# The low parts of the weights in a two-block network: from two engines to VectorE alone

## The chip, the core and the metric

The kernel runs on 1 core of one Trainium2 chip, in one launch. The metric is the device time of one execution in microseconds, as the median of repeated runs. The engines are named as in the profile: PE is TensorE (PEld its weight loads), DVE is VectorE, ACT is ScalarE, POOL is GpSimd, and SP is SyncE, which issues the loads.

## What is computed

Two networks of two layers each, on 256 tokens of width 1024 in float32. The first block's layer has one large input projection and three mixers whose outputs are gated and summed; the second block's layer has two feed-forward parts around a convolution mixer (layer 0) or a latent attention (layer 1), each with an attention over a memory of 256 tokens.

```python
def first_block(x, ...):
    for l in range(DEPTH):
        h = rmsnorm(x, norm_g[l])
        proj = h @ w_in[l]
        (a_q, a_ff, a_fb, a_i, a_g, b_q, b_k, b_v, b_g, c_s, c_g, merge) = jnp.split(proj, IN_OFFSETS, axis=-1)
        y_a = hgrn2_mixer(a_q, a_ff, a_fb, a_i, lbs[l], hgrn_norm_g[l]) * jax.nn.silu(a_g)
        y_b = retention_mixer(b_q, b_k, b_v, ret_norm_g[l], ret_norm_b[l]) * jax.nn.silu(b_g)
        y_c = rwkv7_mixer(c_s, ...) * jax.nn.silu(c_g)
        gates = jax.nn.sigmoid(merge.reshape(b, t, 3, D_MODEL))
        mixed = (gates[:, :, 0] * (y_a @ w_branch_a[l]) + gates[:, :, 1] * (y_b @ w_branch_b[l])
                 + gates[:, :, 2] * (y_c @ w_branch_c[l]))
        x = x + mixed @ w_out[l]
    return rmsnorm(x, final_norm_g)

def second_block(x, mem, ...):
    for layer in range(DEPTH):
        x = x + 0.5 * swiglu(rms_norm(x, norm_g[layer, 0]), ffn_w13[layer, 0], ffn_w2[layer, 0])
        h = rms_norm(x, norm_g[layer, 1])
        # layer 0: short_conv_mixer(h), layer 1: causal_mla_attention; both with memory_attention
        x = x + jnp.concatenate([y_mix, y_mem], axis=-1) @ w_out[layer]
        x = x + 0.5 * swiglu(rms_norm(x, norm_g[layer, 2]), ffn_w13[layer, 1], ffn_w2[layer, 1])
    return x
```

## The kernel before

**Layout.** Activations lie feature by feature: eight blocks of 128 features, 256 tokens each. Every projection runs over the weights in pieces of 128 x 256 features times a token width of 256.

**Three matmuls for one.** A float32 operand is split into a high part (rounded to the format `F32R`) and a low part (what the rounding left), and `mm3` (lines 343 to 347) adds up low x high, high x low and high x high, each a 128x128 by 128x256 matmul. The activations are split once and used by all weights. The weights are split as they arrive.

**The stream of weights.** `wload` (lines 327 to 341) is a generator that `fm` and `tm` (lines 349 and 364) draw on. It loads one chunk of 512 KB from HBM through the SP queue into a tile `raw` (three buffers), and treats it in pieces of 128x512: ScalarE casts the piece to its high part `whi` (line 386), and one of two engines subtracts that from the piece, which gives the low part `wlo` (line 387). A running number `nw` counts the pieces; each third piece is subtracted on GpSimd, the other two on VectorE. The high and low parts have four buffers each in a pool `whi`; in the first block a second pool `whx` of three buffers takes three pieces of each seven. One piece feeds twelve matmuls. Lines 386 and 387 stand in the helper `split`, which also splits activations, always on VectorE.

**What sets the order.** Each engine works through its own list of instructions in order. The kernel records its instructions as generators woven together by `weave` (line 39): in a layer of the first block, projections fill TensorE between the steps of four chains (the operands, the recurrences and the outputs of the third mixer, and the heads of the other two). The framework's scheduler then sets each engine's list when the program is built, by priority and by its own estimate of when an operand is ready; the lists are fixed when the kernel runs. The casts and subtractions of the weights are recorded 80 places ahead (`high_priority(80)`), the recurrences' element-wise steps 50 places ahead (`Ahead`, line 69).

**The chains that the text names.** `hgrn_head` (line 1200) makes the decay products of one head: exponentials on ScalarE, products on VectorE (`Z`, lines 1249 and 1250; `E`, lines 1242 and 1247) and small matmuls (`ppt`, line 1271); GpSimd adds the diagonal blocks into `P` (line 1280), and the matmul `hpo` (line 1181) uses it. `rwkv_states` (line 934) inverts triangular blocks by a chain of small matmuls (`pw`, `px`, lines 1018 and 1026) with VectorE between them (`W`, `XY`), and steps the state (`ch`, lines 1065, 1072 and 1081, with `UV` from VectorE). `bkP` (line 929) and `Pc` (lines 910, 911) are made on GpSimd. `rps` (line 1335) takes the rotated queries and keys `qk` from VectorE. `columns` (line 392) turns sums of squares into reciprocal roots by ten short dependent instructions on VectorE (`rs`, lines 411 to 425, the last on line 430 into `ycol`); `stat` (line 1470) runs it where the second block goes from one part to the next, and TensorE spreads the result (`psn`, line 445). `ffn` (line 1490) holds most of the second block's matmuls; its product `g` on line 1503 reads PSUM.

**Helpers.** Line 80 is the call within `Ahead`, so that many instructions of the recurrences carry this line.

Of the kernel before, what the change touches and what calls it, by code (L numbers as in the profile page):

```python
# [281 lines left out]
class Core:  # L282
# [44 lines left out]
    def wload(s, src, kt, n):  # L327

        nc = s.nc
        raw = s.raw.tile([128, 1024], F32, tag="raw", name="raw")  # L330
        nc.sync.dma_start(out=raw[:, :kt * n], in_=src)
        step = 512 // n
        for j in range(0, kt, step):
            c = min(step, kt - j)
            part = raw[:, j * n:(j + c) * n]
            s.nw += 1
            pool = s.whx if s.whx is not None and s.nw % 7 < 3 else s.whi
            hi, lo = (pool.tile([128, 512], F32R, tag=t, name=t)[:, :c * n] for t in ("whi", "wlo"))
            with s.tc.high_priority(80):
                s.split(hi, lo, part, s.nc.gpsimd if s.nw % 3 == 0 else None)  # L340
            yield j, c, hi.rearrange("p (k n) -> p k n", k=c), lo.rearrange("p (k n) -> p k n", k=c)

    def mm3(s, out, ah, al, bh, bl, start, stop):
# [1490 lines left out]
```

## Time and profile before

| | |
|---|---|
| median of 3 runs | 2808.9 us (2807.02 to 2813.55) |
| the profiled execution | 2819.39 us |
| its span, first to last instruction | 2817.6 us |
| TensorE, matmuls | 2662.0 us, 94% |
| VectorE | 1946.3 us, 69% |
| ScalarE | 1488.4 us, 53% |
| GpSimd | 917.1 us, 33% |
| mean granted clock of TensorE | 0.977 of full speed |
| moved by DMA | 385.41 MB, 137 GB/s |

A busy time is the sum over an engine's instructions, with what runs on top of each other counted once. The first block takes about the first 1770 us (its first layer 0 to 890, its second up to 1770), the second block the rest.

### The profile page before, as it was taken

Reading aid. Unit: us, or ns where it says so; the run is one execution under the profiler, and the core shown is the slowest. Engines: PE = TensorE matmul, PEld = TensorE weight load, DVE = VectorE, ACT = ScalarE, POOL = GpSimd, SP = SyncE. Lnnn points to the kernel's source line nnn. Section 1 sums busy time; section 2 is a strip of 40 time slices with the busy share of each in tenths; the row PEclk is TensorE's granted clock in tenths of the full one; section 3 lists DMA queues with packets and bytes.
Section 4 is the critical chain, followed back from the end, with each engine's and each line's share of the span. In section 5 each row is a group of like instructions: output and inputs, shape, how many; then the busy total and the mean of one; then the engine's idle time right before and its main releaser. Section 6 shows DMA issues by size and latency. Waiting matters only on the chain.

```text
span 2817.6 us, 76691 instructions
## 1 busy us (share of the span) xinstructions
PE 2662.0 (94%) x32003; PEld 2508.6 (89%) x32003; DVE 1946.3 (69%) x4045; ACT 1488.4 (53%) x2964; POOL 917.1 (33%) x868
## 2 busy tenths in 40 slices
PE   7898999999998899899999999999999999999999
PEld 7788888989998788788888999999899999997999
DVE  7878778776666977789776666755665665665654
ACT  6555555544455655555444445645455555545554
POOL 4333333322344433334233235222222322221222
PEclk9999999999999999999999999999999999998999
DMA  5333332333455333332333345555445554542555
GB/s 175 116 104 102 106 99 84 108 118 110 139 168 176 110 121 106 99 103 80 109 124 112 113 145 183 187 172 184 146 165 183 182 177 165 165 147 67 172 182 163
DMA packets 111804, 385.41 MB, mean 137 GB/s; under 512 B 12384, under 2 KB 16992, under 8 KB 111200
## 3 DMA queue, kind: packets, MB, share of 16 engines
q1 hardware_dynamic: 111024, 379.86, 41.7%
q8 instruction: 251, 4.11, 0.6%
q14 instruction: 97, 0.79, 0.1%
q10 hardware_dynamic: 432, 0.64, 0.1%
HBM read 378.36 MB, written 2.10 MB: 135 GB/s over the span
## 4 chain that ended last, share of the span: by engine, by line
PE 64%; DVE 11%; ACT 4%; issue 4%; POOL 3%; DMA 2%; ACTq 0%; POOLq 0%; DVEq 0%
PE pj L345 5%; PE pj L347 4%; PE pj L346 4%; PE pg L345 3%; PE pg L347 3%; PE pg L346 3%; PE pw L345 3%; PE pw L347 3%; PE pw L346 3%; PE pu L345 3%; PE pu L347 3%; PE pu L346 3%; DVE wlo L387 2%; PE pb L345 2%; PE pb L346 2%
## 5 line engine op out<-in xcount | busy, mean ns | idle before, releaser
L386 ACT CAST whi<-raw 128x512 fp32r<-128x512 f32 (+1 forms) x1407 | 858.4, 617 | 819.9 <-PE pj L347 230.7
L387 POOL TENSOR_TENSOR wlo<-raw,whi 128x512 fp32r<-128x512 f32 (+1 forms) x469 | 632.0, 1348 | 1534.2 <-ACT whi L386 1308.4
L387 DVE TENSOR_TENSOR wlo<-raw,whi 128x512 fp32r<-128x512 f32 x938 | 710.2, 762 | 441.1 <-ACT whi L386 436.2
L345 PE MATMUL pj<-hb,wlo 128*128 128x256 f32 x1408 | 431.5, 307 | 3.9 <-DVE wlo L387 1.6
L346 PE MATMUL pj<-hb,whi 128*128 128x256 f32 x1408 | 406.9, 289 | 0.7 <-DVE hb L387 0.7
L347 PE MATMUL pj<-hb,whi 128*128 128x256 f32 x1408 | 405.3, 288 | 0.6 <-issue 0.6
L345 PEld LDWEIGHTS pj<-hb,wlo 128*128 128x128 f32 x1408 | 273.4, 194 | 17.0 <-DVE wlo L387 1.9
L346 PEld LDWEIGHTS pj<-hb,whi 128*128 128x128 f32 x1408 | 274.2, 195 | 3.1 <-DVE hb L387 1.5
L347 PEld LDWEIGHTS pj<-hb,whi 128*128 128x128 f32 x1408 | 273.8, 195 | 2.0 <-issue 0.8
L345 PE MATMUL pg<-hs,wlo 128*128 128x256 f32 x704 | 200.2, 284 | 1.4 <-DVE x L493 1.1
L345 PE MATMUL pu<-hs,wlo 128*128 128x256 f32 x704 | 201.1, 286 | 0.3 <-POOL wlo L387 0.2
L347 PE MATMUL pu<-hs,whi 128*128 128x256 f32 x704 | 200.6, 285 | 0.0
L346 PE MATMUL pu<-hs,whi 128*128 128x256 f32 x704 | 200.4, 285 | 0.0
L345 PE MATMUL pw<-g,wlo 128*128 128x256 f32 x704 | 199.5, 283 | 0.0
L346 PE MATMUL pg<-hs,whi 128*128 128x256 f32 x704 | 199.5, 283 | 0.0
L347 PE MATMUL pg<-hs,whi 128*128 128x256 f32 x704 | 199.4, 283 | 0.0
L346 PE MATMUL pw<-g,whi 128*128 128x256 f32 x704 | 199.2, 283 | 0.0
L347 PE MATMUL pw<-g,whi 128*128 128x256 f32 x704 | 199.2, 283 | 0.0
L345 PE MATMUL pb<-hs,wlo 128*128 128x256 f32 x512 | 150.3, 293 | 1.6 <-DVE gb L847 1.6
L347 PE MATMUL pb<-hs,whi 128*128 128x256 f32 x512 | 145.0, 283 | 0.0
L346 PE MATMUL pb<-hs,whi 128*128 128x256 f32 x512 | 145.0, 283 | 0.0
L345 PEld LDWEIGHTS pu<-hs,wlo 128*128 128x128 f32 x704 | 136.2, 193 | 1.1 <-POOL wlo L387 0.7
(524 smaller groups left out, 7099.7 us busy)
## 6 DMA issues: line engine op xcount, KB each, us to landing
raw<-in_win SPq DMA_DIRECT2D x292, 512.0 KB, 3.6
raw<-in_w SPq DMA_DIRECT2D x256, 512.0 KB, 3.8
raw<-in_wbb SPq DMA_DIRECT2D x32, 512.0 KB, 3.5
raw<-in_wo SPq DMA_DIRECT2D x32, 512.0 KB, 3.6
raw<-in_wconv SPq DMA_DIRECT2D x20, 512.0 KB, 3.5
raw<-in_wba SPq DMA_DIRECT2D x16, 512.0 KB, 3.5
raw<-in_wbc SPq DMA_DIRECT2D x16, 512.0 KB, 3.7
raw<-in_lora SPq DMA_DIRECT2D x16, 256.0 KB, 2.8
```

What stands on the lines that cost most here:

```text
L345: mm(out=out, lhsT=al, rhs=bh, start=start, stop=False)
L346: mm(out=out, lhsT=ah, rhs=bl, start=False, stop=False)
L347: mm(out=out, lhsT=ah, rhs=bh, start=False, stop=stop)
L386: s.nc.scalar.copy(dh, src)
L387: (eng or s.nc.vector).tensor_tensor(dl, src, dh.bitcast(F32), ALU.subtract)
```

## The change

In `wload`, the choice of the engine is dropped: all 1407 subtractions go to VectorE, which `split` uses where no engine is named. The counter `nw` stays, since it also chooses the pool.

```diff
--- before.py
+++ after.py
@@ -337,7 +337,7 @@
             pool = s.whx if s.whx is not None and s.nw % 7 < 3 else s.whi
             hi, lo = (pool.tile([128, 512], F32R, tag=t, name=t)[:, :c * n] for t in ("whi", "wlo"))
             with s.tc.high_priority(80):
-                s.split(hi, lo, part, s.nc.gpsimd if s.nw % 3 == 0 else None)
+                s.split(hi, lo, part)
             yield j, c, hi.rearrange("p (k n) -> p k n", k=c), lo.rearrange("p (k n) -> p k n", k=c)
```

The scheduler sets VectorE's and GpSimd's lists anew. TensorE's list stays as it was, but for shifts by a few matmuls.

VectorE, first layer, at the first head (`Z` and `E` are the head's, `W`, `XY` and `bk` the third mixer's, `g` a gate). Before:

```order
L926 TENSOR_TENSOR bk<-bk,enL 128x8x64
L1247 TENSOR_TENSOR E<-S_991 128x2x4x32
L80 TENSOR_TENSOR W<-pw,c_127 128x256
L387 TENSOR_TENSOR wlo<-raw,whi 128x512
L1249 TENSOR_TENSOR Z<-kf,E 128x2x4x32
L1250 TENSOR_TENSOR Z<-q,E 128x256
L820 SCALAR_TENSOR_TENSOR g<-g,pj 128x512
L80 TENSOR_TENSOR XY<-XY,px 128x256
L1242 TENSOR_TENSOR E<-S_991 128x2x2x64
```

And now:

```order
L926 TENSOR_TENSOR bk<-bk,enL 128x8x64
L1247 TENSOR_TENSOR E<-S_991 128x2x4x32
L80 TENSOR_TENSOR W<-pw,c_127 128x256
L387 TENSOR_TENSOR wlo<-raw,whi 128x512
L1249 TENSOR_TENSOR Z<-kf,E 128x2x4x32
L1250 TENSOR_TENSOR Z<-q,E 128x256
L820 SCALAR_TENSOR_TENSOR g<-g,pj 128x512
L80 TENSOR_TENSOR XY<-XY,px 128x256
L387 TENSOR_TENSOR wlo<-raw,whi 128x512
L80 STREAM_TRANSPOSE XY<-XY 128x256
L1242 TENSOR_TENSOR E<-S_991 128x2x2x64
```

Up to line 1250 the list is the same; the further subtraction stands behind `XY`.

VectorE, second block, the statistics chain before the second feed-forward part of layer 0. Before:

```order
L418 TENSOR_SCALAR rs<-rs 128x2
L387 TENSOR_TENSOR wlo<-raw,whi 128x512
L419 TENSOR_TENSOR rs<-rs 128x2
L420 TENSOR_TENSOR rs<-rs 128x2
L421 SCALAR_TENSOR_TENSOR rs<-rs 128x2
L422 TENSOR_TENSOR rs<-rs 128x2
L423 TENSOR_TENSOR rs<-rs 128x2
L424 TENSOR_SCALAR rs<-rs 128x2
L425 TENSOR_TENSOR rs<-rs 128x2
L430 SCALAR_TENSOR_TENSOR ycol<-rs 128x2
```

And now:

```order
L387 TENSOR_TENSOR wlo<-raw,whi 128x512
L418 TENSOR_SCALAR rs<-rs 128x2
L419 TENSOR_TENSOR rs<-rs 128x2
L420 TENSOR_TENSOR rs<-rs 128x2
L421 SCALAR_TENSOR_TENSOR rs<-rs 128x2
L422 TENSOR_TENSOR rs<-rs 128x2
L387 TENSOR_TENSOR wlo<-raw,whi 128x512
L423 TENSOR_TENSOR rs<-rs 128x2
L424 TENSOR_SCALAR rs<-rs 128x2
L425 TENSOR_TENSOR rs<-rs 128x2
L430 SCALAR_TENSOR_TENSOR ycol<-rs 128x2
```

The chain now holds a second subtraction, between lines 422 and 423; the first moved ahead of line 418.

GpSimd, first layer, from the first `bkP` on. Before:

```order
L929 TENSOR_TENSOR bkP<-bk,Pc 128x512 x2
L387 TENSOR_TENSOR wlo<-raw,whi 128x512
L1171 TENSOR_SCALAR kf<-lf 128x2x256
L387 TENSOR_TENSOR wlo<-raw,whi 128x512 x2
L1221 TENSOR_TENSOR EK<-kf,EK 128x512
L387 TENSOR_TENSOR wlo<-raw,whi 128x512 x2
L1259 TENSOR_TENSOR cm<-cm 128x2x32
L1260 TENSOR_TENSOR cm<-cm 128x2x32
```

And now:

```order
L1171 TENSOR_SCALAR kf<-lf 128x2x256
L929 TENSOR_TENSOR bkP<-bk,Pc 128x512 x2
L1221 TENSOR_TENSOR EK<-kf,EK 128x512
L1259 TENSOR_TENSOR cm<-cm 128x2x32
L1260 TENSOR_TENSOR cm<-cm 128x2x32
```

Five subtractions stood between these instructions; none is left, and `kf` has moved ahead of `bkP`.

## Rows read from the trace of the kernel before

**Rows 1.** The page, busy time of each engine

```profile
PE 2662.0 (94%) x32003; PEld 2508.6 (89%) x32003; DVE 1946.3 (69%) x4045; ACT 1488.4 (53%) x2964; POOL 917.1 (33%) x868
```

**Rows 2.** Stages: length, busy us (instructions) by engine, PEclk, DMA share, GB/s

```profile
0.00:550.00 550.00, 494.30 (x8001) 449.78 (x8002) 442.51 (x1001) 310.40 (x647) 191.47 (x229) 0.96 0.34 111
900.00:1420.00 520.00, 479.52 (x7907) 435.67 (x7906) 429.02 (x946) 302.37 (x630) 188.11 (x209) 0.97 0.33 104
1770.00:2818.00 1048.00, 1015.63 (x8138) 987.98 (x8137) 614.13 (x1214) 546.84 (x1012) 281.15 (x215) 0.98 0.51 164
```

**Rows 3.** What ended waits of PE: us in total, times, longest us

```profile
PE hpo L1181 <- POOL P L1280: 12.5, 7, 3.2
PE pj L345 <- DVE wlo L387: 12.5, 2, 10.9
PE ch L1081 <- DVE UV L80: 8.7, 8, 2.2
PE pw L1018 <- DVE XY L80: 8.1, 9, 2.8
PE psn L445 <- DVE ycol L430: 7.7, 6, 2.9
PE ppt L1271 <- DVE Z L1250: 5.0, 2, 2.5
PE rps L1335 <- DVE qk L1292: 4.9, 3, 2.1
```

**Rows 4.** The page, costliest groups: count, busy us, mean ns, idle before, releaser

```profile
L387 POOL TENSOR_TENSOR wlo<-raw,whi 128x512 fp32r<-128x512 f32 (+1 forms) x469 | 632.0, 1348 | 1534.2 <-ACT whi L386 1308.4
L387 DVE TENSOR_TENSOR wlo<-raw,whi 128x512 fp32r<-128x512 f32 x938 | 710.2, 762 | 441.1 <-ACT whi L386 436.2
```

**Rows 5.** The subtractions: duration in ns min/median/max, first and last start

```profile
L387 POOL TENSOR_TENSOR wlo<-raw,whi x469: 995/1295/4017, 12.0 to 2808.0; 128x512 fp32r<-128x512 f32 x156, 128x384 fp32r<-128x384 f32 x1
L387 DVE TENSOR_TENSOR wlo<-raw,whi x938: 546/692/1807, 10.2 to 2806.5; 128x512 fp32r<-128x512 f32 x187, 128x384 fp32r<-128x384 f32 x1
```

**Rows 6.** Timeline of DVE near the start: start us, us, instruction and count

```profile
26.02 1.89 DVE L387 TENSOR_TENSOR wlo<-raw,whi 128x512 fp32r<-128x512 f32 x3
```

**Rows 7.** Rows 2's first stage, only instructions that read or write wlo

```profile
0.00:550.00 550.00, 256.60 (x833) 163.68 (x833) 110.36 (x141) 100.72 (x70) 0.96 0.34 111
```

**Rows 8.** Lines 1250 and 1503: the group as in rows 4, then as in rows 5

```profile
L1250 DVE TENSOR_TENSOR Z<-q,E 128x256 f32<-128x256 f32 x80 | 41.2, 515 | 1.5 <-ACT E L1245 0.9 <-ACT E L1244 0.5
L1250 DVE TENSOR_TENSOR Z<-q,E x80: 375/417/1490, 90.9 to 1351.6; 128x256 f32<-128x256 f32 x80
L1503 DVE TENSOR_TENSOR g<-si,pu x44: 673/687/690, 1791.2 to 2749.7; 128x512 f32<-128x512 f32 x44
```

**Rows 9.** Timeline of DVE and POOL at three places, as in rows 6

```profile
105.00 1.48 DVE L1250 TENSOR_TENSOR Z<-q,E 128x256 f32<-128x256 f32 x1
104.75 1.44 POOL L387 TENSOR_TENSOR wlo<-raw,whi 128x512 fp32r<-128x512 f32 x1
...
1099.86 3.42 DVE L387 TENSOR_TENSOR wlo<-raw,whi 128x512 fp32r<-128x512 f32 x2
1099.62 3.12 POOL L387 TENSOR_TENSOR wlo<-raw,whi 128x512 fp32r<-128x512 f32 x2
...
2086.41 0.69 DVE L387 TENSOR_TENSOR wlo<-raw,whi 128x512 fp32r<-128x512 f32 x1 [0.84 <-ACT whi L386]
2087.01 0.15 DVE L419 TENSOR_TENSOR rs<-rs 128x2 f32<-128x2 f32 x1
2087.99 1.24 DVE L424 TENSOR_SCALAR rs<-rs 128x2 f32<-128x2 f32 x1
2087.93 1.27 POOL L387 TENSOR_TENSOR wlo<-raw,whi 128x512 fp32r<-128x512 f32 x1 [4.65 <-ACT whi L386]
```

**Rows 10.** What ended waits before the subtractions, as in rows 3

```profile
DVE wlo L387 <- ACT whi L386: 436.2, 363, 4.4
POOL wlo L387 <- ACT whi L386: 1308.4, 351, 25.2
```

## The prediction

> **What bounds the kernel now.** I read four things in this order: the busy times, the stages, the instructions that the change touches, and the waits of TensorE. TensorE is busy for 2662.0 us of a span of 2817.6 us [rows 1], so 155.6 us is all that any edit off TensorE can win, unless it also brings back the granted clock. The windows [rows 2] show where that lies. In the two stretches in which the recurrences of the first block run beside the projections, TensorE is idle for 55.7 us of 550 and 40.5 us of 520, its granted clock is 0.96 and 0.97, and VectorE is busy for 442.5 us (80%) and 429.0 us (83%). In the second block (the last 1048 us) TensorE is idle for only 32.4 us. What to see: TensorE is the bound, and what it loses it loses where VectorE is fullest.
>
> The low parts of the weights are not what TensorE waits for: on them it waited twice, 10.9 of 12.5 us at the start [rows 3]. Its other long waits end on instructions of the recurrences, the attention heads and the statistics: five groups that VectorE releases hold 34.4 us in 28 waits (8.7 + 8.1 + 7.7 + 5.0 + 4.9 us), 1.23 us each, and one that GpSimd's additions to P release holds 12.5 us in 7. So the question is not when a low part is ready, but what its subtraction does to the two in-order queues that feed those waits.
>
> **The change, part by part.** GpSimd loses 469 subtractions of 1348 ns mean, 632.0 us of its 917.1 us; VectorE, which has 938 of them at 762 ns mean, makes 1407 [rows 1, 4].
>
> *What VectorE pays.* One subtraction lasts 692 ns at the median [rows 5], but they overlap at their ends: three in a row took 1.89 us [rows 6], so each further one costs (1.89 - 0.69) / 2 = 0.60 us. 469 x 0.60 = 281 us. Of the 469, 70 fall into the first dense stretch [rows 7].
>
> *What VectorE gets back.* The two engines hold each other up. VectorE's subtractions have a median of 692 ns and a mean of 762, with a longest of 1807 [rows 4, 5]; 938 x 0.070 = 66 us is excess. The product for the heads (line 1250, two operands in SBUF) has a median of 417 and a mean of 515 ns, which gives 80 x 0.098 = 8 us, while the product of line 1503, one operand of which lies in PSUM, never exceeds 690 ns [rows 8]. So the excess is there where both operands are in SBUF. Low end: these two groups alone, 74 us. High end: all of VectorE's 1946.3 us at their rate: 74 us on 938 x 0.692 + 80 x 0.417 = 682 us is 11%, which makes 1946.3 x 0.11 / 1.11 = 193 us. The subtractions are 632.0 of GpSimd's 917.1 us, 69%, so 51 to 133 us goes with them. I take the high end, because short instructions of serial chains are hit by as much as long ones: line 424 took 1.24 us where its neighbour on line 419 took 0.15 [rows 9].
>
> Net, VectorE gains 281 - 133 = 148 us of work and stands at 2094 us, 74% of the span; in the first dense stretch it goes from 442.5 to 442.5 + 70 x (0.60 - 0.28) = 465 us, 84%, the 0.28 being 133 / 469.
>
> The Trainium skill, page "SBUF — State Buffer", section "Who interferes with whom", gives a stricter rule: a VectorE instruction with two SBUF inputs and a GpSimd instruction that reads SBUF exclude each other, and the later one is blocked until the first has finished. By that rule every one of the 469 would cost VectorE half of its 1.295 us median, 0.65 us, if an instruction were always there to be blocked, 304 us in all, and the net would be a gain of 23 us instead of 148 us more work; rows 9 agree with the full block (1.24 us under a GpSimd subtraction of 1.27 us), the means agree with far fewer meetings.
>
> *What of it lies on the path.* Work on VectorE that no TensorE wait follows is hidden by 2662 us of matmuls. What counts is the few microseconds of VectorE's queue ahead of a wait. I read three such places. Ahead of a head's matmuls in the first layer, line 1250 took 1.48 us instead of its 0.417, and GpSimd's subtraction of 1.44 us ran beside it: 1.06 us. Ahead of a step of the recurrence in the second layer, two subtractions took 3.42 us where two at the 0.60 pitch take 1.29: 2.13 us, beside two of GpSimd's in 3.12 us. In a statistics chain of the second block, line 424 lost 1.24 - 0.15 = 1.09 us [rows 9]. So a hit costs 1.06 to 2.13 us there, against 0.60 for a subtraction that joins the queue, and the new order does not put one in everywhere: at the first place none more stands ahead of line 1250, in the statistics chain there is one more. GpSimd's seven waits of 12.5 us carry no such hit that I can name; they stay.
>
> I take it that half of the 28 shown waits carry a hit, of 1.23 us at most (the mean wait, since a wait can't give more than its length): 14 x 1.23 = 17 us. They pay half a subtraction each (one more at one of two places): 28 x 0.5 x 0.60 = 8 us. Net 9 us. The five groups are 34.4 of the 155.6 us of idle time; with the start and GpSimd's 12.5 us set aside, I count another third of that sum as alike, and come to 12 us. Both halves are choices. Low end of the cost: every hit goes and nothing is paid, and the rest of the dense stretches follows, 35 us won. High end: nothing is won at the waits, and the 8 us, scaled alike to 11, are paid.
>
> *Other edits, at nothing.* ScalarE makes the same 1407 high parts. The SP queue issues the same loads, and a raw buffer comes free at the end of a 0.69 us subtraction instead of a 1.3 us one. TensorE's order stays but for shifts of a few matmuls. Low parts are covered now, but for the start, by the weights that TensorE still has ahead of it [rows 3]; if that cover went, each late one would cost up to the 0.60 us.
>
> **The sum.** 2819.4 us for the profiled execution less 12 is 2807. That execution is 0.4% above the median of the runs shown, 2808.9; I set the same 12 us against the median: **2797 us**, 0.4% faster.
>
> **Rivals.**
>
> *Nothing that can be told (0.24).* Where a hit goes, the next instruction that the same matmul needs ends last: a table load or an exponential on ScalarE, or GpSimd's remaining 285 us, which hold VectorE as before. For it: the chains pass through all three engines, and seven waits end on GpSimd already [rows 3]. Against: the waits are short, 1.23 us, and a hit of 1.06 is most of one. Time: 2809. (About 0.2%, 6 us, is what a measurement of this kernel can tell from no change.)
>
> *Slower: VectorE's queue stands (0.22).* A subtraction can't start before ScalarE's cast, which waits for TensorE to release a buffer. VectorE stood before its subtractions for 436.2 us in 363 waits, 1.20 us each, at 39% of the 938; GpSimd stood there 1308.4 us at no cost [rows 10]. With 469 more, 39% of them make 181 further waits, 218 us, and whatever stands behind in VectorE's queue stands too. The place: the statistics chain, where VectorE already waited 0.84 us before a subtraction in the middle of ten dependent instructions [rows 9], and the new order sets one more into that chain. Against: both queues are ordered so that mostly nothing that is ready stands behind. At 80 to 84% of the dense stretches VectorE also has time left to stand in. Price: if one in eight of the 181 is ahead of a TensorE wait, 27 us, less the 12: 2824. It decides from 12 / 218, one in 18.
>
> The Trainium skill, page "Perfetto Trace Analysis", section "Optimizing Scalar/DVE Operations", speaks for this side: handing work to GpSimd can make sense if VectorE is saturated, though the shared port may spoil it. By that rule the change would cost the 27 us if VectorE counted as saturated; at 80 to 84% of the dense stretches the trace does not bear that out.
>
> *A larger gain (0.16).* GpSimd's queue, rid of subtractions that waited 1308.4 us in it, starts its additions, products and gate sums at once; the 12.5 us of waits on P go, as do the hits, and with shorter gaps the granted clock, 0.96 to 0.97 in the dense stretches, rises by a hundredth there (1% of 1070 us, 11 us). 12 + 12.5 + 11 = 35 us: 2774. Against: at those waits GpSimd's own instructions are what runs.
>
> *The change doesn't do what it says* can be left out: no line 387 is left in GpSimd's order.
>
> **How the numbers follow.** Forecast 0.38, larger gain 0.16, nothing 0.24, slower 0.22. Faster by over 0.2% is 0.38 + 0.16 = 0.54, same 0.24, slower 0.22. For the range I leave out some 0.08 of the larger gain below 2772 and some 0.1 of the slower case above 2826: 2772 to 2826. The forecast's own range is 2786 to 2803.
>
> **What would show it.** Right: VectorE's subtractions number 1407 with a mean below 715 ns; its busy time is 2060 to 2130 us; GpSimd's about 285; TensorE's busy time stays at 2662 within 10 us, and its idle time in the dense stretches falls below the 96 us of now; line 424 in the statistics chain is back under 0.2 us. Wrong on the price: VectorE's time before its subtractions goes well beyond 436 us and the waits of TensorE on the statistics and the recurrences grow. Wrong on the cause: the hits go and TensorE's idle time stays at 155 us. A time above 2826 or under 2772 would mean a mechanism that I have not seen.

## The result, and the profile after

The change makes the kernel faster: 2745.3 us (2738.64 to 2755.29) against 2814.1 us (2807.02 to 2818.74), a ratio of 0.9756 with a 95% interval of 0.9738 to 0.9774. That is 69 us, where 12 were forecast, and it lies below the range. The profiled execution took 2752.12 us, with a span of 2750.3.

The page's busy times of the changed kernel and its group of the subtractions, which answer to [rows 1, 4]:

```profile
PE 2649.6 (96%) x32003; PEld 2502.5 (91%) x32003; DVE 2070.4 (75%) x4514; ACT 1489.5 (54%) x2964; POOL 299.1 (11%) x399
...
L387 DVE TENSOR_TENSOR wlo<-raw,whi 128x512 fp32r<-128x512 f32 (+1 forms) x1407 | 983.2, 707 | 419.9 <-ACT whi L386 410.3
```

VectorE makes 1407 low parts and is busy for 124.1 us more; GpSimd is busy for 618 us less. Of the 67.3 us by which the span is shorter, TensorE's busy time gives 12.4 and its idle time 54.9 (155.6 to 100.7).

The stages, cut where TensorE has done the same matmuls, to within one, as in [rows 2] (columns as there):

```profile
0.00:526.70 526.70, 487.57 (x8001) 445.10 (x8002) 449.87 (x1071) 308.84 (x648) 95.94 (x159) 0.97 0.36 115
867.20:1379.50 512.30, 483.33 (x7908) 439.77 (x7908) 428.94 (x1020) 301.67 (x630) 101.86 (x142) 0.96 0.33 107
1721.50:2750.30 1028.80, 1009.56 (x8137) 984.91 (x8136) 696.91 (x1429) 549.55 (x1012) 0.00 (x0) 0.99 0.53 166
```

In the first stage VectorE carries 70 instructions more and is busy for 7.4 us longer; the second has 74 more in the same time. The stages take 23.3, 7.7 and 19.2 us less, and TensorE's idle time in them falls from 55.7 to 39.1, 40.5 to 29.0 and 32.4 to 19.2 us.

What ended waits of TensorE, the lines that answer to [rows 3], and the largest of the others:

```profile
PE hpo L1181 <- POOL P L1280: 13.6, 6, 3.6
PE pj L345 <- DVE wlo L387: 13.4, 4, 10.9
PE pw L1018 <- DVE XY L80: 7.6, 8, 3.2
PE px L1026 <- DVE W L80: 4.7, 5, 1.8
PE pn L453 <- DVE SC L80: 4.3, 4, 2.2
...
PE rps L1335 <- DVE qk L1292: 2.6, 4, 0.8
...
PE ppt L1271 <- DVE Z L1250: 1.8, 2, 1.4
...
PE ch L1081 <- DVE UV L80: 0.8, 1, 0.8
...
PE psn L445 <- DVE ycol L430: 0.3, 2, 0.2
```

`UV`, `ycol`, `Z` and `qk` gave back much of what they held, but `XY` and `P` hardly anything. These rows are only a part of it, and [rows 3] is a choice from its view: four groups that VectorE releases stand in the same view, as long as those chosen.

```profile
PE psn L405 <- DVE acc L468: 8.1, 6, 4.6
PE px L1026 <- DVE W L80: 7.5, 12, 1.6
PE pn L453 <- DVE SC L80: 7.2, 6, 2.1
PE psc L967 <- DVE SC L80: 4.9, 2, 2.6
```

Over all rows of this view that VectorE releases, it is 115.0 us in 116 waits before (38 rows) and 56.1 us in 62 waits now (29 rows).

Timeline at the three places of [rows 9]. First layer, at the first head:

```profile
97.91 1.20 DVE L387 TENSOR_TENSOR wlo<-raw,whi 128x512 fp32r<-128x512 f32 x1
99.02 1.26 DVE L1249 TENSOR_TENSOR Z<-kf,E 128x256 f32<-128x256 f32 x1
100.20 0.41 DVE L1250 TENSOR_TENSOR Z<-q,E 128x256 f32<-128x256 f32 x1
...
97.49 2.51 POOL L929 TENSOR_TENSOR bkP<-bk,Pc 128x512 f32<-128x512 f32 x2 [1.89 <-ACT bk L925]
```

Line 1250 is back at 0.41 us. But the same happens one instruction earlier, under `bkP`: GpSimd's remaining instructions hold VectorE as its subtractions did. In the second layer two subtractions take 1.29 us again, and in the statistics chain line 424 takes 0.17, with a further subtraction among the ten dependent instructions:

```profile
1063.23 1.29 DVE L387 TENSOR_TENSOR wlo<-raw,whi 128x512 fp32r<-128x512 f32 x2
...
2029.30 0.69 DVE L387 TENSOR_TENSOR wlo<-raw,whi 128x512 fp32r<-128x512 f32 x1
2029.91 0.15 DVE L423 TENSOR_TENSOR rs<-rs 128x2 f32<-128x2 f32 x1
2030.09 0.17 DVE L424 TENSOR_SCALAR rs<-rs 128x2 f32<-128x2 f32 x1
```

VectorE's own waits before the subtractions, which answer to [rows 10], are more in number and no longer in sum, though it makes half as many again:

```profile
DVE wlo L387 <- ACT whi L386: 410.3, 525, 3.8
```

### The profile page after: what moved, and what is told of

It reads as the page before. It is cut to its first block, busy times and chain, and to the rows that moved or that the text cites. A ratio compares the mean times of both kernels' runs of the same rounds, so it can differ in the third digit from the quotient of the medians.

```text
span 2750.3 us, 76068 instructions
## 1 busy us (share of the span) xinstructions
PE 2649.6 (96%) x32003; PEld 2502.5 (91%) x32003; DVE 2070.4 (75%) x4514; ACT 1489.5 (54%) x2964; POOL 299.1 (11%) x399
## 4 chain that ended last, share of the span: by engine, by line
PE 75%; DVE 14%; ACT 4%; DMA 3%; issue 2%; POOL 2%; SPq 0%; ACTq 0%; DVEq 0%; POOLq 0%
PE pj L345 7%; PE pj L347 6%; PE pj L346 6%; PE pg L345 4%; PE pg L347 4%; PE pg L346 4%; DVE wlo L387 4%; PE pw L345 3%; PE pw L347 3%; PE pw L346 3%; PE pu L347 3%; PE pu L345 3%; PE pu L346 3%; PE pb L345 2%; PE pb L346 2%
## 5 line engine op out<-in xcount | busy, mean ns | idle before, releaser
L387 DVE TENSOR_TENSOR wlo<-raw,whi 128x512 fp32r<-128x512 f32 (+1 forms) x1407 | 983.2, 707 | 419.9 <-ACT whi L386 410.3
L345 PEld LDWEIGHTS pg<-hs,wlo 128*128 128x128 f32 x704 | 135.7, 193 | 2.6 <-issue 2.1
L346 PEld LDWEIGHTS pg<-hs,whi 128*128 128x128 f32 x704 | 135.8, 193 | 2.2 <-DVE hs L474 2.2
```

What stands on the lines that cost most here:

```text
L345: mm(out=out, lhsT=al, rhs=bh, start=start, stop=False)
L346: mm(out=out, lhsT=ah, rhs=bl, start=False, stop=False)
L387: (eng or s.nc.vector).tensor_tensor(dl, src, dh.bitcast(F32), ALU.subtract)
```

## The experiments

Three theories stood at the start. **A, the hold:** a long GpSimd instruction that reads SBUF stops VectorE's instructions with two operands there, and those stops cost the 69 us. **B, the queue:** GpSimd's own additions and products stood behind 632 us of subtractions, and a third of the low parts came late. **C, the order:** VectorE's new list is simply a better one. Ratios are against the kernel before on the same chip; a gain in us is what the ratio falls short of 1, times 2814. The chips differ by a few us, so a time as measured and a ratio can give slightly different sums.

**1. The hold taken out, the queue kept.** Diff against the kernel before; a call of `third` stands where `wload` called `split`, here and below.

```diff
+def third(s, hi, lo, part):
+    if s.nw % 3:
+        return s.split(hi, lo, part)
+    s.nc.scalar.copy(hi, part)
+    s.nc.gpsimd.tensor_tensor(lo[:, 0:8], part[:, 0:8], hi[:, 0:8].bitcast(F32), ALU.subtract)
+    s.nc.gpsimd.memset(lo[:, 8:].bitcast(F32), 0.0)
+    s.nc.gpsimd.memset(lo[:, 8:].bitcast(F32), 0.0)
```

> The kernel before, with one thing taken out: GpSimd's 469 subtractions read 128x512 of raw and whi no more. For each third piece GpSimd makes a subtraction of 128x8 (so that it waits for the same cast) and then two memsets of the rest of wlo, about 0.2 + 2 x 0.53 us, as long as the old 1.3 us. So the low part of every third piece is left out of the result but for 8 columns. Lists, waits, buffers and VectorE's work stay as before. Theory A (the hold: GpSimd's long reads stop VectorE's instructions with two operands in SBUF, and that cost the 69 us): VectorE's subtractions come to a mean under 715 ns on their 938, VectorE's busy time falls by 100 us or more to about 1800 us, and the time is 2735 to 2765 us. Theory B (the queue: GpSimd's own additions to P, gate sums and products stand behind 632 us of subtractions that wait for casts, and low parts come late): nothing changes, 2805 to 2822 us. Theory C (the new order of VectorE's list is simply a better one): the list is the old one, 2805 to 2822 us.

Measured: 2722.5 us, ratio 0.9657 (0.9635 to 0.9679), a gain of 97 us. Its busy times and subtractions:

```profile
PE 2632.0 (97%) x32003; PEld 2484.6 (91%) x32003; DVE 1782.5 (66%) x4045; ACT 1490.1 (55%) x2964; POOL 866.4 (32%) x1806
...
L387 DVE TENSOR_TENSOR wlo<-raw,whi 128x512 fp32r<-128x512 f32 x938 | 658.3, 705 | 484.6 <-ACT whi L386 468.6
```

GpSimd is as busy as before within 51 us, VectorE has the same 4045 instructions, and they take 163.8 us less: that is the hold. TensorE's idle time falls to 84.2 us, its waits on VectorE to 50.3 us in 57 (26 rows), and its busy time by 30.0 us, with the mean granted clock at 0.987 instead of 0.977. The time is 13 us under theory A's range; B and C, which saw no change, fall for the bulk of it. That the list is the old one can be read from the trace: VectorE's instructions run in the order of the kernel before, but for 17 small differences, mostly neighbours that changed places.

One thing besides the hold is not as before: `raw` comes free after the 128x8 subtraction, while the memsets still run. ScalarE's waits on the loads `in_w` and `in_win` fall from 75.1 us (45.9 + 29.2) to 33.2 (10.8 + 9.9 + 6.9 + 5.6). TensorE hardly waits for parts of the weights in either (14.8 and 13.6 us), but how much of the 97 us this gave was not tried apart; run 4 bears on it.

**2. No low part for the third pieces at all,** against the kernel before:

```diff
+def third(s, hi, lo, part):
+    if s.nw % 3 == 0:
+        s.nc.scalar.copy(hi, part)
+        return hi
+    s.split(hi, lo, part)
+    return lo
```

> The kernel before with the low part of every third piece left out: nobody makes it, and the matmul that should use it reads the high part a second time, so TensorE's work is the same. This is the changed kernel without the 469 subtractions on VectorE (some 281 us of VectorE's time). It prices what VectorE's further work costs. If that work costs what the sum at the waits said (about 8 to 11 us), the time is 2734 to 2738 us; if it costs nothing, within 5 us of the changed kernel's 2745 us; if the gain of the hold was much larger and mostly paid back, below 2725 us. Theories A and B both expect 2725 to 2750 us here; theory C (order alone) does not say.

Measured: 2716.2 us, 0.9638 (0.9615 to 0.9661), a gain of 102 us; VectorE is busy for 1776.4 us. It is not told apart from run 1, although GpSimd's queue is empty here (281.3 us). So the changed kernel, 0.9756, gives back 0.0099 to 0.0118, or 28 to 33 us, for 288 to 294 us of further work on VectorE. Here too `raw` comes free early (34.9 us of waits on the two loads, 62.9 in the changed kernel), so the work alone may have cost less.

**3 and 4. The hold put back, and the same without reading,** both against the changed kernel:

```diff
+def third(s, hi, lo, part):
+    s.split(hi, lo, part)
+    if s.nw % 3 == 0:
+        s.nc.gpsimd.tensor_tensor(part, part, hi.bitcast(F32), ALU.subtract)
```

```diff
+        s.nc.gpsimd.tensor_copy(part[:, 0:1], hi[:, 0:1].bitcast(F32))
+        s.nc.gpsimd.memset(part, 0.0)
+        s.nc.gpsimd.memset(part, 0.0)
```

> The changed kernel, with a subtraction on GpSimd added after VectorE's for every third piece: raw = raw - whi in place, which nobody reads. GpSimd has again 469 instructions of 128x512 that read two operands in SBUF; VectorE still makes all 1407 low parts. A raw buffer comes free some 1.3 us later. Theory A: the hold is back, and VectorE has its further 281 us too: VectorE's subtractions have a mean of 750 ns or more, and the time is 2805 to 2850 us. Theory B: GpSimd's queue is full again but no low part is late, 2770 to 2815 us. Theory C: near 2745 us.

> As the run with the added subtraction, but what GpSimd does on every third piece is a copy of one column and two memsets of the same part of raw, about 0.3 + 2 x 0.53 us, which write and hardly read. The queue of GpSimd and the release of raw are as in that run. Theory A: no hold to speak of, VectorE's subtractions stay at a mean of 700 to 715 ns, 2740 to 2765 us. Theory B: the same time as the run with the added subtraction, within 8 us. Theory C: near 2745 us in both.

Measured: 2902.7 us, 1.0295 (1.027 to 1.032), and 2786.9 us, 0.9890 (0.9865 to 0.9916). The busy times and subtractions of the first, then the busy times of the second:

```profile
PE 2696.6 (93%) x32003; PEld 2536.5 (87%) x32003; DVE 2331.7 (80%) x4514; ACT 1481.7 (51%) x2964; POOL 962.9 (33%) x868
...
L387 DVE TENSOR_TENSOR wlo<-raw,whi 128x512 fp32r<-128x512 f32 (+1 forms) x1407 | 1136.4, 821 | 336.8 <-ACT whi L386 330.8
```

```profile
PE 2653.5 (96%) x32003; PEld 2504.1 (90%) x32003; DVE 2072.6 (75%) x4514; ACT 1483.7 (53%) x2964; POOL 924.8 (33%) x1806
```

GpSimd is about as busy in both, but reading makes VectorE's same 4514 instructions 261.3 us longer than in the changed kernel and writing 2.2 us. The time differs by 114 us, for 259.1 us of hold: 0.44 a us, in two runs that both release `raw` late. Yet theory A missed both times, by 53 and 22 us above its ranges. The writing run shows 38 us (0.0134) that are no hold. Two groups of ScalarE's waits on loads, now that `raw` comes free after GpSimd's memsets, are 124.6 us, and 62.9 in the changed kernel (41.9 + 21.0):

```profile
ACT whi L386 <- DMA raw<-in_w: 73.2, 55, 3.0
...
ACT whi L386 <- DMA raw<-in_win: 51.4, 39, 4.5
```

**5. The queue alone.** So GpSimd was given work that keeps no shared buffer, against the changed kernel (`scr` is a tile of 128x64 of its own):

```diff
+        s.nc.gpsimd.tensor_copy(s.scr[:, 0:1], hi[:, 0:1].bitcast(F32))
+        for _ in range(7):
+            s.nc.gpsimd.memset(s.scr, 0.0)
```

> The changed kernel, with work for GpSimd that touches no shared buffer for long: for each third piece a copy of one column of whi and seven memsets of 128x64 on a tile of its own, about 0.3 + 7 x 0.15 us. It asks where the 41 us come from by which the run with memsets on raw was slower than the changed kernel. If they came from the raw buffer, which came free later there (casts waited 125 us for loads, against some 60), this run is at 2740 to 2758 us; if GpSimd's own instructions are late behind the memsets (theory B), it is at 2775 to 2795 us again.

Measured: 2753.7 us, 0.9774 (0.9744 to 0.9804), not told apart from the changed kernel. The busy times and GpSimd's two groups:

```profile
PE 2643.3 (96%) x32003; PEld 2495.4 (91%) x32003; DVE 2070.9 (75%) x4514; ACT 1488.0 (54%) x2964; POOL 1034.5 (38%) x4151
```

```profile
L1843 POOL MEMSET scr<- 128x64 f32 x3283 | 503.0, 153 | 186.5
L1841 POOL COPY scr<-whi 128x1 f32<-128x1 f32 x469 | 249.0, 531 | 1277.9 <-ACT whi L386 1277.0
```

GpSimd is busier than in the kernel before (1034.5 to 917.1 us), its list again stands for 1277.0 us before casts (1308.4 then), and no loss can be told. VectorE's list has the order of the changed kernel's, instruction by instruction. Nor did low parts from GpSimd come late in the kernel before, but for 1.0 us:

```profile
PE pj L345 <- POOL wlo L387: 0.8, 1, 0.8
PE pu L345 <- POOL wlo L387: 0.2, 1, 0.2
```

Theory B falls. What run 4 lost goes with the late `raw`: the two groups of waits on loads are 35.3 + 30.1 = 65.4 us here. That is an argument, since VectorE's list in run 4 differs from the changed kernel's in some 160 places. If it holds, 61.7 us more of these waits cost 38 us there, and the 41.9 us fewer in run 1 would be some 26 of its 97 us, an estimate from this one pair. The hold would then be worth 71 / 163.8 = 0.43 a us, close to the 0.44 of runs 3 and 4.

**6 and 7. One block at a time.** Against the kernel before; the second run has `is None`.

```diff
-                s.split(hi, lo, part, s.nc.gpsimd if s.nw % 3 == 0 else None)
+                s.split(hi, lo, part, s.nc.gpsimd if s.nw % 3 == 0 and s.whx is not None else None)
```

> The kernel before, with each third piece subtracted on GpSimd in the first block only (254 pieces); the second block's 215 go to VectorE. Theory A (hold), with what the two traces show: from the first matmul of the second block to the end it took 1049.4 us before and 1030.6 us changed, so 18.8 us should go, 2795 us (2788 to 2802). Rival: what one block wins the other takes back (a fuller VectorE list in the second block also holds up what follows), 2805 us or more.

> The kernel before, with each third piece subtracted on GpSimd in the second block only (215 pieces); the first block's 254 go to VectorE. Theory A: the first block got 48.6 us shorter by the change, so 2766 us (2759 to 2773). Together with the run that undoes the other block the two gains should add up to the whole 69 us. Rival: the gain comes from the queue of GpSimd, whose own instructions all stand in the first block; then this run has the whole gain, 2745 us, and the other has none.

Measured: 2797.0 us, 0.9933 (0.9911 to 0.9954), and 2767.1 us, 0.9812 (0.9798 to 0.9827). GpSimd made 253 and 216 subtractions in the traces, one off the numbers expected. The gains, 19 and 53 us, add up to 72 against 69. Both blocks win, the second too, where GpSimd has no instructions of its own.

**8 and 9. More or fewer of them on GpSimd:** `s.nw % 6`, then `s.nw % 2` in the same line.

> The kernel before with each sixth piece, not each third, subtracted on GpSimd (234 of 1407). If the price is proportional to the holds, half of the way goes: 2814 - 34 = 2780 us (2773 to 2787). If a few subtractions already spoil most of the chains (or the first half costs nothing), 2800 us or more (2755 us or less).

> The kernel before with every second piece subtracted on GpSimd (703 of 1407). By the two prices: VectorE's excess rises from 164 to about 164 x 703 / 469 = 246 us, +82 x 0.59 = +48 us; VectorE has 234 subtractions less, 234 x 0.61 x 0.09 = -13 us: 2814 + 35 = 2849 us (2835 to 2865). Rival: relief of a VectorE that is 80 to 83% full in the dense stretches is worth more than that there, 2814 us or less.

Measured: 2788.2 us, 0.9893 (0.9863 to 0.9923), and 2853.4 us, 1.0122 (1.0095 to 1.0149). With 0, 234, 469 and 703 subtractions on GpSimd the ratios are 0.9756, 0.9893, 1 and 1.0122. The half is within 5 us of the sum of the two prices; the sixth is 1 us beyond its range as measured, and within it by its ratio (2784 us). By the ratios the steps cost 39, 30 and 34 us, so the net price of a subtraction on GpSimd is close to proportional.

**10 to 12. A version that beats both.** Against the changed kernel: first `bkP`, `EK` and the gate sums to VectorE, then the rest of the two blocks' instructions as well (`ar`, `Pc`, `UV`, `ks`, `kf`, `cm`, `P`, `onr`, `ro`), then of these `UV`, the second layer's `kf` and `ro` to ScalarE instead. The first, and one line of each of the others:

```diff
-            nc.gpsimd.tensor_tensor(mixed[:, sl, :], mixed[:, sl, :], t, ALU.add)
+            nc.vector.tensor_tensor(mixed[:, sl, :], mixed[:, sl, :], t, ALU.add)
-            G.tensor_tensor(bkP[:, d], bk[:, d, :, 0:2, :],
+            V.tensor_tensor(bkP[:, d], bk[:, d, :, 0:2, :],
-        nc.gpsimd.tensor_tensor(EK, kf, EK, ALU.mult)
+        nc.vector.tensor_tensor(EK, kf, EK, ALU.mult)
...
-            nc.gpsimd.tensor_tensor(dst, dst, cm[i * 32:i * 32 + 32, :, 0, :], ALU.add)
+            nc.vector.tensor_tensor(dst, dst, cm[i * 32:i * 32 + 32, :, 0, :], ALU.add)
...
-            V.tensor_copy(UV[o:o + 64, 1, :, h, :], UV[o:o + 64, 0, :, h, :])
+            A.copy(UV[o:o + 64, 1, :, h, :], UV[o:o + 64, 0, :, h, :])
```

> The changed kernel, with three more kinds of instruction taken from GpSimd and given to VectorE: the gate sums (line 848, 32 of 128x512), bkP (line 929, 32 of 128x512) and EK (line 1221, 16 of 128x512). In the changed kernel VectorE's instructions that run beside these last 43 us longer in sum than alone. Theory A at the prices measured so far (97 us of time for 164 us of VectorE's excess, 0.59 a us; 23 to 29 us for 288 us of further subtractions, 0.08 to 0.10 a us): -25 + 80 x 0.61 x 0.1 = -20 us, 2725 us. Rival (VectorE is full): the dense stretches have VectorE at 84 to 85%, and each further us there costs up to 0.6: no gain or a loss, 2745 to 2775 us.

> The changed kernel, with all of GpSimd's remaining work in the two blocks but the memsets given to VectorE (the three kinds above and P, cm, UV, ar, Pc, ks, kf, onr, ro). VectorE's excess beside GpSimd, 59 us, goes; some 110 us of short instructions come. Theory A: -35 + 11 = -24 us, and of the 13.6 us in which TensorE waited for P some 8 go: 2713 us (2705 to 2725). Rival (VectorE is full in the first block): 2745 to 2790 us.

> The run in which VectorE takes GpSimd's remaining work, but UV (line 958), kf of the second layer (line 1168) and the scale and shift of ro (line 1369), 80 instructions, go to ScalarE instead. If further work on VectorE costs 0.1 a us, 80 x 0.3 us less give 2 to 3 us, 2713 us (2706 to 2718); if ScalarE's list, on which the exponentials of the heads stand, takes it worse, 2720 to 2735 us.

Measured: 2732.2 us, 0.9696 (0.9674 to 0.9718); 2715.5 us, 0.9630 (0.9616 to 0.9644); 2723.7 us, 0.9670 (0.9640 to 0.9699). The first moves 80 instructions onto VectorE, and its busy time goes from 2070.4 to 2074.7 us only; it gains 17 of the 20 us expected. The second is the fastest of these, 35 us below the changed kernel by the ratios and 2 us from the 2713 expected. ScalarE in VectorE's place wins nothing; whether it loses is not told apart, since the intervals touch. The second's busy times, its subtractions (min/median/max in ns) and what TensorE waits for at `hpo`:

```profile
PE 2631.3 (97%) x32003; PEld 2484.9 (92%) x32003; DVE 2110.5 (78%) x4874; ACT 1491.5 (55%) x2968; POOL 11.9 (0%) x39
```

```profile
L387 DVE TENSOR_TENSOR wlo<-raw,whi x1407: 548/692/695, 10.2 to 2703.2; 128x512 fp32r<-128x512 f32 x175, 128x384 fp32r<-128x384 f32 x1
```

```profile
PE hpo L1181 <- DVE P L1280: 10.2, 7, 3.6
```

With 11.9 us of work left on GpSimd, none of the 1407 subtractions is longer than 695 ns; the longest of the kernel before took 1807 [rows 5]. The waits on `P` stay when VectorE makes it, so it was not late for being made on GpSimd; what does make it late was not tried.

## Why the prediction was wrong in size

The direction and the cause were right: the hold was what the change took away, and each sign of the forecast's case came, but for TensorE's busy time, which fell by 12.4 us where 10 were allowed. The size of the gain is what failed.

*What VectorE pays:* 281 us forecast; between run 1 and the changed kernel 2070.4 - 1782.5 = 287.9 us, 0.614 each. Right.

*What VectorE gets back:* 51 to 133 us, 133 taken; 163.8 us measured by run 1. Too small, and outside my bounds: the rate of two groups was spread over all lines as if they met GpSimd alike. On the two groups run 1 shows 57.4 us (51.9 + 5.5) where 51 were taken, on all else 106.4 where the high end had 82. The reading that the excess is there where both operands are in SBUF was too narrow as well: line 424, one of the three places, reads a single tensor. The net, 124 us, came out within 24 us of the 148.

*What of it lies on the path* is the step that failed: "half of the 28 shown waits carry a hit, of 1.23 us at most", with another third as alike, 23 us of gain against 11 us of cost. Run 1 shows 97 us of gain, run 2 with the changed kernel up to 33 us of cost. I had read five groups of waits, 34.4 us, and taken them for the body of what VectorE makes TensorE wait for. The view has 38 such groups, 115.0 us in 116 waits, 25 of the groups under 3 us each; without the hold 50.3 us are left. The five were a choice, with groups of 8.1, 7.5, 7.2 and 4.9 us left out, and the choice was scaled up by a third instead of by the sum.

The sum alone would not have mended the forecast. By its own rule, half of 115.0 us would be won (57.5) and half a subtraction paid at each of 116 waits (34.8), 23 us net. At these waits run 1 shows 64.7 us won, so "half" was near; but from run 1 to the changed kernel they grow by 5.8 us only, so the payment was far too high. And two terms stood at nothing: of run 1's span, 101.4 us shorter, 6.7 are other idle time of TensorE and 30.0 its busy time, at a higher granted clock (a part of that is scatter, as the last section shows). The forecast had the clock only in the larger-gain rival, at 11 us.

*In the chain's terms:* 163.8 us of hold were worth 97 us, 0.59 a us with the earlier release of `raw` in it (0.44 by runs 3 and 4, without); 288 us of subtractions cost 28 us, some 0.10 a us or less. My sum had used 23 / 133 = 0.17 and 11 / 281 = 0.04. Why a stop costs four to six times as much as planned work of the same length was not tried apart. An argument, no more: a stopped instruction was ready and stands in some chain, while a planned one can be set where the list waits anyway, 410.3 us before the subtractions alone.

*The rivals.* Nothing: what else the matmuls wait for did not end at the same time; TensorE's waits on ScalarE rose only from 14.7 to 17.1 us. Slower, VectorE's queue stands: its wait before subtractions fell from 436.2 to 410.3 us. The larger gain had the wrong mechanism: its 12.5 us of waits on `P` stayed at 13.6, and run 5 shows the freed queue to be worth nothing that can be told. Its clock term, 11 us in the dense stretches, is near the 12.4 us of the whole kernel by luck: in the two stretches the granted clock went from 0.96 to 0.97 and from 0.97 to 0.96, and TensorE's busy time fell by 6.7 and rose by 3.8 us.

*The rule of the skill.* The measured 163.8 us lie between the trace's 51 and the 304 us that were estimated by the rule of the Trainium skill, page "SBUF — State Buffer", section "Who interferes with whom", for the case that an instruction is always there to be blocked. The same section says that only GpSimd instructions that read SBUF exclude VectorE's two-input ones; the trace agrees, with 261.3 us for reading and 2.2 and 0.5 us for writing (runs 3, 4 and 5).

## What to carry to other kernels

When two engines hold each other up, price the stop by an experiment that keeps the queue and drops the reads, and watch what else it changes (here, when `raw` comes free): a us of unplanned stop was worth 0.44 to 0.59 us here and a us of planned work some 0.10 or less, so work may well move onto the fuller engine. Before the path term is summed, add up all rows of the waits that one engine releases; the five chosen were under a third of them. And when the move pays, look for what else on the freed engine still holds the other: the rest of GpSimd's work was worth another 35 us.

## What was not expected of the hardware

A GpSimd instruction that reads SBUF can stop a VectorE instruction however small that is: `rs` of 128x2 took 1.24 us under a subtraction of 1.27 [rows 9]. Nor need it have two tensors to read: line 424 has one, and so has line 418, whose 52 instructions of 128x4 were shorter in run 1 too (the kernel before, then run 1):

```profile
L418 DVE TENSOR_SCALAR rs<-rs 128x4 int32<-128x4 int32 x52 | 16.9, 325 | 0.9
L418 DVE TENSOR_SCALAR rs<-rs 128x4 int32<-128x4 int32 x52 | 11.3, 217 | 0.8
```

Writing does not stop VectorE: 3283 memsets on GpSimd, 503.0 us, left its 4514 instructions at 2070.9 us against 2070.4.

And TensorE's busy time is no constant of its 32003 matmuls: it was 2696.6 (run 3), 2662.0 (before), 2649.6 (changed) and 2632.0 us (run 1) at mean granted clocks of 0.966, 0.977, 0.979 and 0.987. A part of that is scatter: seven executions of the kernel before on one chip, beside runs 5, 8 and 9, had clocks from 0.976 to 0.984, and spans from 2822.9 down to 2805.6 us. The medians of the executions beside run 1 still rise, from 0.978 to 0.9855. That the shorter waits raised the clock, and so paid twice, was not tried apart.
